# Down projection of an encoder layer: its DMA transfers put in an order written out by hand

## The chip, the core and the metric

The kernel runs on one core of a Trainium2 chip. The core has five engines with a queue of instructions each: TensorE (PE: matmuls, with its weight loads shown apart as PEld), VectorE (DVE), ScalarE (ACT), GpSimd (POOL) and SyncE (SP). SyncE computes nothing here; it issues DMA transfers, which a set of 16 DMA engines then carries out. The metric is the time of the whole program on the device in microseconds (us), lower is better. The kernel is built with a framework of tiles: the program says which tile an operation reads and writes, and a scheduler orders the instructions of each engine and places the semaphores. Where the program calls `tc.keep_in_program_order`, the scheduler keeps an instruction at its place in the program, relative to the others that are kept.

## The reference, cut to what matters

One layer of a streaming encoder on 512 prompt frames, 16 meta tokens and 64 sample frames, model width 2048, all in float32. The attention half (two head groups side by side, one output projection) is not touched here. What the change concerns is the second half:

```python
h = rmsnorm(x, lp['norm_ffn_g'])
x = x + (jax.nn.silu(h @ lp['ffn_w_gate']) * (h @ lp['ffn_w_up'])) @ lp['ffn_w_down']
...
y_prompt = rmsnorm(xp[:, N_META:], final_norm_g)
y_sample = rmsnorm(xs, final_norm_g)
```

Gate and up weights are 2048 x 5632, the down weights 5632 x 2048. After attention 576 tokens are left (`TQ`), which the kernel holds as two halves of 288 (`QH`).

## The kernel before, in words

*Number format.* A float32 product is made of three products of rounded parts (fp32r): each operand is split into a high part and a low part, and hi·hi, hi·lo and lo·hi are added up. A split takes ScalarE (copy to the high part: L156 for weights, L1185 for token operands) and then VectorE (what is left: L153 for weights, L1187 for operands).

*Seven products for eight.* The three big matmuls of the feed-forward use `winograd` (L998): blocks of 2 x 2 quarters are multiplied with 7 products, each of a sum of weight quarters (`ws`, L1025: some on GpSimd, one on VectorE) with a sum of token quarters. In the order `CHAIN` the first product takes a weight quarter as it is, so it needs only the two splits of `raw`. For each product TensorE runs `bh·wh` and `bl·wh` at L1056 and `bh·wl` at L1060. `wh` and `wl` have two buffers each, so ScalarE and VectorE prepare one product while TensorE runs another.

*Gate and up.* The loop `for u in range(FC // 2)` takes 22 units of 256 hidden columns. For each unit and each of gate and up, two weight pieces of 1 MB (`raw`) are loaded and the products are summed up in a tile `c` of the pool `fb`. At the end of a unit GpSimd multiplies gate and up (L1245, two instructions), the result is stored to DRAM (`actspill`, two stores of 288 KB), and for all units but the last two GpSimd also forms the four sums of quarters that the down projection needs, which are stored to `sumspill`.

*Down projection.* The 22 units are its contraction dimension, taken in `blocks = [4, 4, 4, 4, 4, 2]`. For each of the first five blocks there are 8 steps `d`, one for 256 output columns: `down_rows` loads a weight piece of 1 MB (`raw`, pool `fr`, two buffers), runs the 7 products (28 operands of 144 KB in all, held in SBUF in the pool `bc`), and VectorE adds each product into the accumulators `y` (L1295), which start with the residual, loaded from `x2spill` in the first block, two per step. The sixth block multiplies plainly (`plain_rows`), and behind it `finish` (two halves) normalises and turns the result: squares, the constant-setting of `vc`, a reciprocal root (`vc`, `rc`, L167 to L169), transposes on TensorE, scaling into `ot` by VectorE (L1348) or ScalarE (L1346), and the stores of the outputs.

*The operands of the next block.* `builder` (L1158) is a generator. It fetches operands `bl` from `actspill` and `sumspill`, a given number ahead, and converts them in two steps, ScalarE first, VectorE then. `down_rows` advances it once per product, so that three and a half operands become ready per step `d`, and a block's 28 during the block before. For the first block the same generator (`start`) is advanced by the last unit's "up" products; it is set to run 4 fetches ahead. What is left of it is drained behind the loop of units.

*What sets the order.* All loads and stores go through SyncE's one queue (L137, L140). From `pinned[0] = True` on (down projection), splits, sums and conversions are kept in program order by `pin`; the DMA transfers are not: the scheduler decides which goes first on SyncE's queue. The pool `yp`, from which the down projection takes `wh`, `wl` and `ws`, and the pool `yy` of the accumulators lie in memory that the gate/up pools (`fb`, `rw`, `fw`) give back, so that the first tiles of the down projection wait until the stores of the last `c` have read it.

Of the kernel before, what the change touches and what calls it, by code (L numbers as in the profile page):

```python
# [11 lines left out]
F32 = mybir.dt.float32  # L12
# [103 lines left out]
def encoder_step(  # L116
# [16 lines left out]

    S.preload_act_table_set("natural_log_exp_and_others")

    def load(dst, src):
        nc.sync.dma_start(dst, src)  # L137

    def store(dst, src):
        nc.sync.dma_start(dst, src)  # L140

    def const(name, shape, src):
        t = cp.tile(shape, F32, name=name)
# [844 lines left out]
    def load_raw(pool, src, r0, nk, c0, bufs, tag="raw"):  # L988
        r = pool.tile([P, nk, 256], F32, name="raw", tag=tag, bufs=bufs)
        load(r, src[r0:r0 + nk * P, c0:c0 + 256].rearrange("(k p) c -> p k c", p=P))  # L990
        return r
# [166 lines left out]
    def builder(m0, count, plain, ahead, by_product=False):  # L1158

        srcs = {}  # L1160
        for m in range(m0, m0 + count):
            quarter = [actspill[2 * m + f, :, c] for f in range(2) for c in (slice(0, QH), slice(QH, TQ))]
            if plain:
                for p, src in zip((1, 2, 4, 5), quarter):
                    srcs[m, p] = src
            else:
                for p, src in zip(ORDER, (quarter[0], quarter[2], sumspill[m, :, 2], sumspill[m, :, 0],
                                          sumspill[m, :, 1], quarter[3], sumspill[m, :, 3])):
                    srcs[m, p] = src
        order = [p for p, _ in CHAIN]  # L1170
        todo = sorted(srcs, key=lambda mp: order.index(mp[1])) if by_product else list(srcs)

        def fetch(n):
            for m, p in todo[n:n + 1]:
                hi = bc.tile([P, QH], F32R, name=f"bh{p}_{m % 8}")
                lo = bc.tile([P, QH], F32R, name=f"bl{p}_{m % 8}")
                load(f32(lo), srcs[m, p])
                operands[m % 8, p] = (hi, lo)

        for n in range(ahead):  # L1180
            fetch(n)
        for n, (m, p) in enumerate(todo):
            fetch(n + ahead)
            hi, lo = operands[m % 8, p]
            pin(S.activation(hi, f32(lo), AF.Copy))  # L1185
            yield
            pin(V.tensor_tensor(lo, f32(lo), f32(hi), op=ALU.subtract))  # L1187
            yield
# [14 lines left out]
            G.tensor_tensor(g[:, f, :], g[:, f, :], rb2, op=ALU.mult)  # L1203

    blocks = [4, 4, 4, 4, 4, 2]

    turn = 0
    norm = token_norm()
    start = builder(0, blocks[0], False, 4, True)
    for u in range(FC // 2):  # L1210
        out = {}
        for which, wsrc in (("g", w_gate), ("u", w_up)):
            first = turn == 0
            raws = []
            for hf in range(2):
                if turn:
                    rp, bufs = (rw, 1) if turn % 3 == 0 else (fr, 2)
                    raws.append(load_raw(rp, wsrc, hf * 1024, 8, u * 256, bufs))
                turn += 1
            c = fb.tile([P, 2, TQ], F32, name="c", tag="c" + which, bufs=2)  # L1220
            chain = () if first else CHAIN if u == FC // 2 - 1 and which == "u" else WIDE
            take = combined(*quarters(c[:, 0, :], c[:, 1, :]), chain)
            done = [0]

            def step():
                if u == 0 and which == "u":
                    next(norm, None)
                if u == FC // 2 - 1 and which == "u":
                    done[0] += 1
                    if done[0] > 2:  # L1230
                        for _ in range(2 * blocks[0]):
                            next(start, None)

            if first:
                winograd(fw, fb, raws, range(4, 8), take, banks0, step=step)
            else:
                winograd(fw, fb, raws, range(8), take, step=step, chain=chain)
            out[which] = c
            if u and which == "g":
                gated(c)  # L1240
        g, w = out["g"], out["u"]
        if u == 0:
            gated(g)
        for f in range(2):
            G.tensor_tensor(w[:, f, :], w[:, f, :], g[:, f, :], op=ALU.mult)  # L1245
            if u < FC // 2 - 1:
                store(actspill[2 * u + f], w[:, f, :])
        if u < FC // 2 - blocks[-1]:
            b11, b12, b21, b22 = quarters(w[:, 0, :], w[:, 1, :])
            t = g.rearrange("p f (h c) -> p (f h) c", h=2)  # L1250
            G.tensor_tensor(t[:, 0, :], b12, b11, op=ALU.subtract)
            G.tensor_tensor(t[:, 1, :], b22, t[:, 0, :], op=ALU.subtract)
            G.tensor_tensor(t[:, 2, :], b21, t[:, 1, :], op=ALU.subtract)
            G.tensor_tensor(t[:, 3, :], b22, b12, op=ALU.subtract)
            store(sumspill[u], t)
    for _ in start:
        pass
    for f in range(2):
        store(actspill[FC - 2 + f], out["u"][:, f, :])
    close_fb()  # L1260
    close_rw()
    yy, close_yy = pool("yy", "right")
# [23 lines left out]
                done(2 * d + f, h)  # L1286

    def down_rows(m0, n, d, slots, step):
        raws = [load_raw(fr, w_down, m0 * 256, 2 * n, d * 256, 2)]
        y11, y12, y21, y22 = quarters(y[2 * d], y[2 * d + 1])  # L1290
        parts = {1: (y11,), 5: (y22,), 6: (y12,), 2: (y11,), 7: (y22,), 3: (y12,), 4: (y21,)}

        def take(p, banks):
            for c in parts[p]:
                V.tensor_tensor(c, c, banks[p], op=ALU.add)  # L1295

        winograd(yp, yp, raws, slots, take, step=step, chain=CHAIN)
# [15 lines left out]
    def finish(h, ahead):  # L1313

        groups = [(q, j) for q in range(4) for j in range(3)]

        def turned(q, j):  # L1320
            o, n = tok[h][j]
            ps = pmt()
            for k in range(4):
                PE.transpose(ps[0:n, k * P:(k + 1) * P], y[q * 4 + k][:, o:o + n], ident)
            return ps

        held = []
        for g in groups[:ahead]:
            held.append(turned(*g))
            yield  # L1330
        pc = pmt()
        vc = yp.tile([P, 3], F32, name=f"vc{h}")
        rc = yp.tile([P, 3], F32, name=f"rc{h}")
        V.memset(vc, 1.0)
        for j, (o, n) in enumerate(tok[h]):
            PE.matmul(pc[0:n, 2 * j:2 * j + 2], sqs[h][:, o - h * QH:o - h * QH + n], ones[:, 0:2],
                      start=True, stop=True)
            V.tensor_scalar(vc[0:n, j:j + 1], pc[0:n, 2 * j:2 * j + 1], 1.0 / D, EPS, op0=ALU.mult, op1=ALU.add)
        rsqrt(rc, vc)
        yield  # L1340
        for i, (q, j) in enumerate(groups):
            o, n = tok[h][j]
            ps = held.pop(0) if held else turned(q, j)
            ot = yp.tile([P, 512], F32, name="ot", tag="ot", bufs=OT_BUFS)
            if i % 2:
                S.activation(ot[0:n], ps[0:n, :], AF.Copy, scale=rc[0:n, j:j + 1])  # L1346
            else:
                V.tensor_scalar(ot[0:n], ps[0:n, :], rc[0:n, j:j + 1], None, op0=ALU.mult)  # L1348
            cs = slice(q * 512, (q + 1) * 512)
            if o == 0:  # L1350
                store(y_sample[:, cs], ot[0:NS])
            else:
                store(y_prompt[o - NS:o - NS + n, cs], ot[0:n])
            yield

    pinned[0] = True
    first = 0
    for bi, n in enumerate(blocks):
        slots = [(first + k) % 8 for k in range(n)]
        if bi + 1 < len(blocks):  # L1360
            build = builder(first + n, blocks[bi + 1], bi + 2 == len(blocks), 4)

            def step():
                next(build, None)

            for d in range(KC // 2):
                if bi == 0:
                    for i in (2 * d, 2 * d + 1):
                        y.append(yy.tile([P, TQ], F32, name=f"y{i}"))
                        load(y[i], x2spill[i])  # L1370
                down_rows(first, n, d, slots, step)
            for _ in build:
                pass
        else:
            before = iter(())
            for h in range(2):
                for d in range(KC // 2):
                    plain_rows(first, n, d, (h,), slots, squares)
                    if d:
                        for _ in range(2):  # L1380
                            next(before, None)
                before = finish(h, 5 * h)
            for _ in before:
                pass
        first += n
# [78 lines left out]
```

## Time and profile before

| | us |
|---|---|
| the runs | 2552.08, 2550.22, 2552.07; median 2552.07 |
| the profiled execution | 2555.87 |
| span of its trace | 2554.1 |
| of it TensorE busy | 2452.2 |
| VectorE busy | 1800.2 |
| ScalarE busy | 1108.3 |
| GpSimd busy | 738.8 |

The span runs from the first to the last instruction on record; what lies around it (1.8 us) is start and end of the program. "Busy" counts an engine's computing instructions; DMA issues, semaphores and branches are left out. A group row of the page (`L1056 PE MATMUL m<-bh,wh ...`) names line, engine, operation, output and inputs, shapes and count, then busy time, the mean of one in ns, and the idle time just before such instructions with what ended it. A row of DMA issues names the transfer, the queue (`SPq` is SyncE's), its count, size, and the median time from issue to landing. In a timeline a row has the time from the start of the span, the duration, engine, line, operation, tiles and count; in square brackets stands how long the engine had waited and for what. The mean granted clock of TensorE was 0.986 of full speed in this execution.

### The profile page before, as it was taken

How to read it: one execution, taken by the hardware profiler on the slowest of the kernel's cores; microseconds unless marked ns; L12 is line 12 of the kernel's file. 1: busy time of each engine (PE TensorE's matmuls, PEld its weight loads, DVE VectorE, ACT ScalarE, POOL GpSimd, SP SyncE). 2: the span in 40 equal slices, each digit the busy share in tenths (PEclk: the TensorE clock that was granted, in tenths of full speed). 3: DMA queues.
4: the chain of work that ended last, by engine and by line, in shares of the span. 5: the costliest groups of instructions: out<-in, count | busy, mean ns of one | idle time of the engine just before them, and what ended most of it. 6: DMA issues, size and time to landing. Idle time of an engine off the chain costs nothing. (4 is left out here: it accounts for less than half of the span.)

```text
span 2554.1 us, 44879 instructions
## 1 busy us (share of the span) xinstructions
PE 2452.2 (96%) x17847; PEld 2393.5 (94%) x17847; DVE 1800.2 (70%) x2825; ACT 1108.3 (43%) x2008; POOL 738.8 (29%) x614
## 2 busy tenths in 40 slices
PE   6999999998999999999999999999999899999997
PEld 5999999987999888999999999999999899999997
DVE  5455555556555567877777777777777899899975
ACT  5233433334344444444444444444445444444445
POOL 0000000000000165554545445454543222222236
PEclk9999999999999899999999999999999899999999
DMA  6433223334232453343333334333335542452334
GB/s 205 123 92 97 80 80 85 86 87 140 88 96 84 140 157 124 118 137 116 121 104 127 128 118 137 114 121 105 128 127 166 201 153 83 151 162 83 108 102 149
DMA packets 330564, 307.73 MB, mean 120 GB/s; under 512 B 24708, under 2 KB 298507, under 8 KB 330355
## 3 DMA queue, kind: packets, MB, share of 16 engines
q1 hardware_dynamic: 330354, 304.87, 38.1%
q8 instruction: 140, 2.29, 0.4%
q14 instruction: 70, 0.57, 0.1%
HBM read 250.82 MB, written 56.68 MB: 120 GB/s over the span
## 5 line engine op out<-in xcount | busy, mean ns | idle before, releaser
L1056 PE MATMUL m<-bh,wh 128*128 128x288 f32 x3584 | 969.5, 296 | 13.4 <-DMA bl<-actspill 9.6
L1056 PE MATMUL m<-bl,wh 128*128 128x288 f32 x3584 | 969.0, 295 | 0.0
L1056 PEld LDWEIGHTS m<-bh,wh 128*128 128x128 f32 x3584 | 674.9, 188 | 14.4 <-ACT wh L156 14.3
L1056 PEld LDWEIGHTS m<-bl,wh 128*128 128x128 f32 x3584 | 678.6, 189 | 0.1
L1060 PE MATMUL m<-bh,wl 128*128 128x288 f32 x3584 | 586.4, 299 | 18.3 <-DVE wl L153 15.7
L1060 PEld LDWEIGHTS m<-bh,wl 128*128 128x128 f32 x3584 | 512.6, 189 | 32.3 <-DVE wl L153 31.3
L1025 POOL TENSOR_TENSOR ws<-raw 128x512 f32<-128x512 f32 x256 | 342.5, 1346 | 607.2 <-DVE wl L153 352.6
L156 ACT ACTIVATE wh<-ws 128x512 fp32r<-128x512 f32 (+1 forms) x340 | 288.8, 849 | 449.2 <-PE m L1056 300.4
L153 DVE TENSOR_TENSOR wl<-ws,wh 128x512 fp32r<-128x512 f32 (+1 forms) x340 | 379.9, 1117 | 114.1 <-ACT wh L156 113.6
L153 DVE TENSOR_TENSOR wl<-raw,wh 128x512 fp32r<-128x512 f32 x416 | 403.8, 985 | 27.1 <-ACT wh L156 17.2
L156 ACT ACTIVATE wh<-raw 128x512 fp32r<-128x512 f32 x416 | 249.7, 626 | 308.0 <-PE m L1056 279.3
L108 PE MATMUL ps<-xh,wh 128*128 128x296 f32 x992 | 229.3, 313 | 6.5 <-ACT wh L156 6.5
L108 PE MATMUL ps<-xl,wh 128*128 128x296 f32 x992 | 219.0, 302 | 0.0
L108 PE MATMUL ps<-xh,wl 128*128 128x296 f32 x992 | 218.7, 302 | 0.0
L108 PEld LDWEIGHTS ps<-xh,wh 128*128 128x128 f32 x992 | 163.4, 192 | 10.7 <-ACT wh L156 6.7
L108 PEld LDWEIGHTS ps<-xl,wh 128*128 128x128 f32 x992 | 164.1, 192 | 0.0
L108 PEld LDWEIGHTS ps<-xh,wl 128*128 128x128 f32 x992 | 163.8, 192 | 0.3 <-DVE wl L153 0.3
L1025 DVE TENSOR_TENSOR ws<-ws,raw 128x512 f32<-128x512 f32 x128 | 92.4, 722 | 87.4 <-POOL ws L1025 81.1
L153 DVE TENSOR_TENSOR wl<-wr,wh 128x1024 fp32r<-128x1024 f32 (+1 forms) x110 | 117.8, 1071 | 45.2 <-ACT wh L156 43.3
L1295 DVE TENSOR_TENSOR y<-y,m 128x288 f32<-128x288 f32 x280 | 125.5, 448 | 20.1 <-PE m L1060 18.8
L156 ACT ACTIVATE wh<-wr 128x1024 fp32r<-128x1024 f32 (+1 forms) x110 | 101.7, 929 | 80.3 <-PE ps L108 72.0
L1203 POOL TENSOR_TENSOR c<-c,rb 128x576 f32<-128x576 f32 x44 | 73.0, 1661 | 165.5 <-ACT c L1202 163.0
(363 smaller groups left out, 3330.2 us busy)
## 6 DMA issues: line engine op xcount, KB each, us to landing
raw<-in_ffn_w_gate SPq DMA_DIRECT2D x44, 1024.0 KB, 6.6
raw<-in_ffn_w_up SPq DMA_DIRECT2D x44, 1024.0 KB, 5.2
raw<-in_ffn_w_down SPq DMA_DIRECT2D x40, 1024.0 KB, 5.4
wr<-in_w_in SPq DMA_DIRECT2D x60, 512.0 KB, 4.0
actspill<-c SPq DMA_DIRECT2D x44, 288.0 KB, 2.1
sumspill<-c SPq DMA_DIRECT2D x20, 576.0 KB, 2.8
bl<-sumspill SPq DMA_DIRECT2D x80, 144.0 KB, 3.4
bl<-actspill SPq DMA_DIRECT2D x68, 144.0 KB, 3.8
```

What stands on the lines that cost most here:

```text
L108: self.tc.keep_in_program_order(self.pe.matmul(out, lhsT, rhs, start=start, stop=stop))
L153: V.tensor_tensor(lo, src, f32(hi), op=ALU.subtract)
L156: S.activation(hi, src, AF.Copy)
L1025: engine.tensor_tensor(w[:, k:k + m, :], pick(xs), pick(ys), op=op)
L1056: PE.matmul(banks[p], wh[:, k, :], x, start=first and new and k == 0 and x is hi, stop=False, skip_group_check=not new)
L1060: PE.matmul(banks[p], wl[:, k, :], hi, start=False, stop=last and k == n - 1, skip_group_check=not new)
L1203: G.tensor_tensor(g[:, f, :], g[:, f, :], rb2, op=ALU.mult)
L1295: V.tensor_tensor(c, c, banks[p], op=ALU.add)
```

## The change

- `load` and `store` become one function `transfer`, which keeps a transfer in program order on SyncE's queue while `paced[0]` is set. It is set at the first product of the last unit's "up" matmul and taken back at the beginning of the last block.
- The weight pieces of the down projection are asked for by `fetch_raw`, ahead of the step that uses them: the first within the last unit, the second behind the last operand of the first block, and each further one behind step `d - 2`. `down_rows` takes the piece from the dictionary `fetched`.
- `start` fetches 8 operands ahead instead of 4, in two groups of four: the first two steps of the last unit's "up" products each ask for one group.
- The last unit's two stores to `actspill` are issued by GpSimd (`G.dma_start`) instead of SyncE.
- The accumulators `y` are loaded four at the first step and then two per step, two steps ahead of their use.
- The constant-setting of `vc` in `finish` is kept in program order.

The arithmetic, its order on TensorE, and the sizes of the buffers stay as they are.

```diff
...
-    def load(dst, src):
-        nc.sync.dma_start(dst, src)
-
-    def store(dst, src):
-        nc.sync.dma_start(dst, src)
+    paced = [False]
+
+    def transfer(dst, src):
+        ins = nc.sync.dma_start(dst, src)
+        if paced[0]:
+            tc.keep_in_program_order(ins)
+
+    load = store = transfer
...
         for n in range(ahead):
             fetch(n)
+            if by_product and n % count == count - 1:
+                yield
         for n, (m, p) in enumerate(todo):
...
     blocks = [4, 4, 4, 4, 4, 2]
+    fetched = {}
+
+    def fetch_raw(m0, n, d):
+
+        fetched[m0, d] = load_raw(fr, w_down, m0 * 256, 2 * n, d * 256, 2)
 
     turn = 0
     norm = token_norm()
-    start = builder(0, blocks[0], False, 4, True)
+    start = builder(0, blocks[0], False, 2 * blocks[0], True)
...
                 if u == FC // 2 - 1 and which == "u":
                     done[0] += 1
+                    if done[0] == 1:
+                        paced[0] = True
+                        fetch_raw(0, blocks[0], 0)
+                    if done[0] < 3:
+                        next(start)
                     if done[0] > 2:
                         for _ in range(2 * blocks[0]):
                             next(start, None)
...
     for _ in start:
         pass
+    fetch_raw(0, blocks[0], 1)
     for f in range(2):
-        store(actspill[FC - 2 + f], out["u"][:, f, :])
+        G.dma_start(actspill[FC - 2 + f], out["u"][:, f, :])
...
     def down_rows(m0, n, d, slots, step):
-        raws = [load_raw(fr, w_down, m0 * 256, 2 * n, d * 256, 2)]
+        raws = [fetched.pop((m0, d))]
...
-        V.memset(vc, 1.0)
+        pin(V.memset(vc, 1.0))
...
+    def accumulator(i):
+        y.append(yy.tile([P, TQ], F32, name=f"y{i}"))
+        load(y[i], x2spill[i])
+
...
             for d in range(KC // 2):
-                if bi == 0:
-                    for i in (2 * d, 2 * d + 1):
-                        y.append(yy.tile([P, TQ], F32, name=f"y{i}"))
-                        load(y[i], x2spill[i])
+                if bi == 0 and d == 0:
+                    for i in range(4):
+                        accumulator(i)
+                if bi == 0 and 2 * d + 4 < KC:
+                    for i in (2 * d + 4, 2 * d + 5):
+                        accumulator(i)
                 down_rows(first, n, d, slots, step)
+                if d + 2 < KC // 2:
+                    fetch_raw(first, n, d + 2)
+                elif bi + 2 < len(blocks):
+                    fetch_raw(first + n, blocks[bi + 1], d + 2 - KC // 2)
             for _ in build:
                 pass
         else:
+            paced[0] = False
             before = iter(())
...
```

## The prediction

> **What bounds the kernel now.** I read the page first (busy shares, the slices, the groups), then the table of stretches over the down projection, then the timelines of the queues and engines where a stretch loses time.
>
> ```profile
> span 2554.1 us, 44879 instructions
> PE 2452.2 (96%) x17847; PEld 2393.5 (94%) x17847; DVE 1800.2 (70%) x2825; ACT 1108.3 (43%) x2008; POOL 738.8 (29%) x614
> L1056 PE MATMUL m<-bh,wh 128*128 128x288 f32 x3584 | 969.5, 296 | 13.4 <-DMA bl<-actspill 9.6
> raw<-in_ffn_w_down SPq DMA_DIRECT2D x40, 1024.0 KB, 5.4
> actspill<-c SPq DMA_DIRECT2D x44, 288.0 KB, 2.1
> bl<-sumspill SPq DMA_DIRECT2D x80, 144.0 KB, 3.4
> ```
>
> TensorE is the bound: 96% busy. Of the 13.4 us that it waits ahead of the first product of a group, 9.6 are one wait. The stretches place it:
>
> ```profile
> 1957.00:1978.00 21.00, 21.00 (x160) 21.00 (x160) 20.55 (x39) 16.41 (x36) 3.69 (x2) 1.00 0.88 263
> 1978.80:1984.10 5.30, 0.01 (x1) 0.00 (x0) 2.61 (x2) 0.41 (x1) 2.29 (x2) 1.00 0.96 312
> 1984.10:1988.40 4.30, 0.00 (x0) 0.00 (x0) 1.67 (x6) 2.17 (x6) 0.41 (x1) 0.50 0.70 236
> 1988.40:1997.80 9.40, 8.38 (x33) 8.04 (x34) 6.13 (x9) 2.55 (x5) 3.36 (x3) 0.50 0.96 331
> 1997.80:2003.60 5.80, 5.80 (x46) 5.80 (x45) 5.11 (x9) 3.20 (x6) 1.29 (x1) 1.00 0.30 105
> 2182.90:2196.90 14.00, 11.97 (x85) 11.26 (x85) 10.47 (x20) 5.32 (x10) 2.55 (x2) 1.00 0.66 209
> 2196.90:2365.00 168.10, 161.93 (x1177) 157.03 (x1178) 156.72 (x274) 78.50 (x148) 36.85 (x28) 1.00 0.36 113
> ```
>
> The columns are stretch, length, busy time of TensorE, its weight loads, VectorE, ScalarE and GpSimd, granted clock, DMA share, GB/s. Between the last unit and the first step of the down projection TensorE stands still for 9.6 us, then runs 9.4 us at half clock (33 products recorded, where 5.8 us at full clock hold 46). In the steady part VectorE, 156.7 of 168.1 us, is nearly as full as TensorE: 14 steps of 12.0 us. One step, 2182.9 to 2196.9, took 14.0. So three places can move: the seam, that step, and whatever the new queue order makes late.
>
> **The seam.** Timelines of SyncE's queue, GpSimd, ScalarE, TensorE and VectorE there:
>
> ```profile
> 1975.90 0.38 SPq L137 DMA_DIRECT2D raw<-in_ffn_w_down  x1
> 1976.38 3.79 SPq L137 DMA_DIRECT2D bl<-sumspill  x4
> 1980.27 1.27 SPq L140 DMA_DIRECT2D actspill<-c  x2
> ...
> 1978.02 3.07 POOL L1245 TENSOR_TENSOR c<-c 128x576 f32<-128x576 f32 x2 [14.37 <-issue]
> ...
> 1978.85 0.41 ACT L1131 ACTIVATE c<-m 128x288 f32<-128x288 f32 x1 [0.20 <-PE m L1060]
> 1985.10 1.54 ACT L1185 ACTIVATE bh<-bl 128x288 fp32r<-128x288 f32 x4 [5.84 <-DMA bl<-sumspill]
> 1987.76 0.63 ACT L156 ACTIVATE wh<-raw 128x512 fp32r<-128x512 f32 x1 [1.13 <-DMA actspill<-c]
> ...
> 1988.44 0.61 PE L1056 MATMUL m<-bh,wh 128*128 128x288 f32 x1 [9.63 <-DMA bl<-actspill]
> 1991.70 0.61 PE L1060 MATMUL m<-bh,wl 128*128 128x288 f32 x1 [0.97 <-DVE wl L153]
> ...
> 1977.80 3.60 DVE L1187 TENSOR_TENSOR bl<-bl,bh 128x288 fp32r<-128x288 f32 x3
> 1985.57 1.58 DVE L1187 TENSOR_TENSOR bl<-bl,bh 128x288 fp32r<-128x288 f32 x4 [4.17 <-ACT bh L1185]
> ```
>
> The wait is put down to an operand, but ScalarE's rows tell what came last: the first weight split (1987.76) waits until the last unit's products `c` have been stored, since `wh` of the new pool lies where `c` was. The second store was issued at about 1981.1 and landed at about 1987.7: 6.6 us, where such stores take 2.1 by the page. Ahead of it on the queue stood a weight piece of 1 MB and four operands; those too landed late (1985.1).
>
> **The change, part by part, against the profiled execution (2555.87 us).**
>
> *Stores on GpSimd's queue, block 1's operands and the second weight piece behind block 0's operands.* The order of instructions in the changed kernel: multiplication, store, multiplication, store on GpSimd; ScalarE's last copy of `c` now stands behind two of the last four conversions. Without the weight piece these operands, released at 1976 as now, land some 2.2 to 3.4 us later, so the copy ends near 1979.6 instead of 1979.26. First multiplication done at 1979.55 (half of 3.07). No row shows a store issued by GpSimd; SyncE's two took 0.64 each at this place, and I take that, from 0.3 to 2.1 (a whole landing). The second multiplication runs 1980.2 to 1981.75, 0.65 later than before; its issue ends at 1982.4. Landing: 2.1 at best, 6.6 at worst if it again waits its turn; the weight piece, now issued near 1978 and landing 5.4 later at 1983.4, is still being moved, so I take 2.1 plus some 0.4: 1984.9. The split starts 2.9 us earlier than at 1987.76. Ends: 4.5 earlier (no delay, 2.1) to 1.5 later. Behind the split nothing comes sooner: the operands then land near 1980.5, GpSimd's sum and VectorE's subtraction wait for the same stores. **-2.9 (-4.5 to +1.5).**
>
> For the store's price the Trainium skill has a figure (DMA: Bandwidth & Descriptors, Anatomy of one DMA, SWDGE path): about 2.0 us plus bytes over 436 GB/s per DMA of GpSimd, by which I estimate 2.7 us for 288 KB and the seam at -2.7; no run here shows it yet.
>
> *Half clock.* The wait stays near 6.7 us, and the clock had been cut 5.3 us into it. It came back 9.4 after the restart, 6.1 after the second wait (1991.70). I keep 9.4. If the clock comes back 3.4 us sooner or later (the length that 1984.1 to 1997.8, 13.7, holds four times), half of it counts: **0 (-1.7 to +1.7).**
>
> *The step of 14.0 us.* Its rows:
>
> ```profile
> 2182.90 0.38 SPq L137 DMA_DIRECT2D raw<-in_ffn_w_down  x1
> 2183.37 2.90 SPq L137 DMA_DIRECT2D bl<-sumspill  x3
> ...
> 2186.38 0.63 ACT L156 ACTIVATE wh<-raw 128x512 fp32r<-128x512 f32 x1 [0.63 <-PE m L1056]
> 2188.02 0.63 ACT L156 ACTIVATE wh<-ws 128x512 fp32r<-128x512 f32 x1 [1.01 <-PE m L1056]
> 2191.81 0.44 ACT L1185 ACTIVATE bh<-bl 128x288 fp32r<-128x288 f32 x1 [3.15 <-DMA bl<-sumspill]
> ...
> 2192.82 0.69 DVE L1025 TENSOR_TENSOR ws<-ws,raw 128x512 f32<-128x512 f32 x1 [3.25 <-POOL ws L1025]
> ```
>
> A cluster of operands surrounded the weight piece; both came late, ScalarE and VectorE waited. In the new order three or four operands follow each piece and none is in flight ahead of it. Back to 12.0: **-2.0 (-2.0 to 0).** The weight pieces themselves come no earlier: there are two buffers in both kernels, and a piece already leaves when its buffer is free (2182.90, 2196.89); "two steps ahead" is what the trace shows already. That part counts 0.
>
> *First operands of a block.* The scheduler used to load them before the block began. Pinned, they stand behind the weight piece issued at a block's start, and the first conversion follows in the same step. ScalarE gets there 4.1 us into the step (2186.38 + 0.63 - 2182.90). The operand leaves 0.5 in. By its own 3.4 it lands at 3.9 and costs nothing; behind the piece (5.4) at some 6.0; at worst as above, 8.9. At 6.0 two conversions of 0.43 push the next split from 5.1 to 6.9; TensorE wants its 0.63 us finished at about 7.0, late by 0.5. Four blocks (the first has the seam's slack): **+2.0 (0 to 8.2, four times the 2.05 of the step above).**
>
> *Tail.* The constant-setting of `vc` is pinned, and the scheduler puts two weight splits behind the normalisation and two output scalings:
>
> ```profile
> 2515.93 0.68 DVE L153 TENSOR_TENSOR wl<-raw,wh 128x512 fp32r<-128x512 f32 x1
> 2516.53 0.15 DVE L169 SCALAR_TENSOR_TENSOR rc<-vc,rc 128x3 f32<-128x3 f32 x1
> 2516.72 1.40 DVE L1348 TENSOR_SCALAR ot<-m,rc 64x512 f32<-64x512 f32 x2
> ```
>
> One split moves behind 1.40 us of scalings; transposes moved forward on TensorE cover most: **+0.4 (-0.6 to +1.4).** The loads of `y`, spread over the steps, cost nothing: each is due two steps, 24 us, later. Without that cover a pair would add about its 1.1 us of issue and landing.
>
> Sum: -2.9 + 0 - 2.0 + 2.0 + 0.4 = **-2.5 us**; ends -8.8 and +12.8. The profiled execution, 2555.87, is 3.8 above the median 2552.07; taken from the median: **2549.6 us.**
>
> **The rivals.**
>
> *The seam closes further* (faster). Store landed at the low end (-4.5), clock back one length sooner (-1.7), the long step gone (-2.0), the block starts hidden because VectorE sets the pace there anyway (0): -8.2, 2543.9. For it: 156.7 of 168.1 on VectorE, so a late ScalarE split has some room; against it: the new store sits in line on GpSimd between two multiplications.
>
> *Operands late at each block's start* (slower). One mechanism: ScalarE takes its work in order, and a conversion waiting for its operand holds every weight split behind it. At 3.15 per block, the wait in the row of 2191.81, four cost 12.6 instead of 2.0: +8.1, 2560.2. With the rest as forecast it decides from 2.4 a block. Against: other weight pieces land within 5.4, which leaves most of a split's slack.
>
> *The stores are no quicker on the other queue.* They need the same DMA engines, and the weight piece is still under way: landing 6.6 again, at 1989.0, so +1.2 at the seam, sum +1.6, 2553.7. For it: 312 GB/s in that stretch, DMA share 0.96. Against: the new order takes a megabyte and thirteen operands from ahead of them.
>
> *VectorE holds the stores up.* Its three subtractions beside the multiplications took 3.60, 1.2 each, against 1.58 for four afterwards: the two engines get in each other's way. If GpSimd must wait for VectorE's last subtractions before a store can go, and these end near 1983, the store lands 1.5 later: sum -1.0, 2551.1. The Trainium skill (SBUF — State Buffer, SBUF: two separate sides) warns of just that: GpSimd's DMA descriptors cannot be written while VectorE holds the shared port in a fast mode. Whether these subtractions use that mode no run here shows.
>
> **How the numbers follow.** Chances: forecast 0.37, further closing 0.34, late operands 0.18, stores no quicker 0.07, VectorE in the way 0.04. I take 0.2%, 5.1 us, as what can be told from no change. The first, fourth and fifth lie within it: 0.48; faster 0.34; slower 0.18. The range reaches down past the rival to the sum's lower end, 2552.07 - 8.8 = 2543, and up to where slower begins, 2557, which leaves out the 0.18.
>
> **What would show it.** Right: the wait ahead of the first product of the down projection near 6.7 us, ended by a store of GpSimd's, its first weight split 2.9 us closer behind the last unit; the half-clock stretch still there; no step of 14 us; short waits of ScalarE for operands at block starts. Wrong: the half clock gone, GpSimd's issue or landing much over 3 us, waits for operands of 2 us or more in four steps, or steps that differ from 12.0 throughout.

## The result, and the profile after

Over 11 runs each the changed kernel takes 2558.66 us in the median, the kernel before 2552.63. The ratio is 1.0022, with a 95% interval of 1.0014 to 1.0030: by the ratio 5.6 us slower, between 3.6 and 7.7. The forecast was 2.5 us faster (2549.6 us, from 2543 to 2557). The profiled execution took 2559.38 us.

The page of the changed kernel has nearly the same busy times as before:

```profile
span 2557.1 us, 44837 instructions
PE 2449.7 (96%) x17847; PEld 2390.5 (93%) x17847; DVE 1800.2 (70%) x2825; ACT 1106.9 (43%) x2008; POOL 739.8 (29%) x616
L1059 PE MATMUL m<-bh,wh 128*128 128x288 f32 x3584 | 968.4, 296 | 13.1 <-ACT wh L159 9.7
bl<-sumspill SPq DMA_DIRECT2D x80, 144.0 KB, 5.0
```

TensorE's waits ahead of the first products of a group come to 13.1 us in place of 13.4, 9.7 of them now put down to weight splits, and the operands take 5.0 us to land where they took 3.4. The stretches of the changed kernel (columns as in the prediction): seam, the start of the fourth block, and the end from the thirteenth weight piece of the last block on:

```profile
1978.90:1983.90 5.00, 0.15 (x2) 0.00 (x0) 4.41 (x5) 1.52 (x4) 3.96 (x4) 1.00 0.89 295
1983.90:1986.10 2.20, 0.00 (x0) 0.00 (x0) 0.00 (x0) 0.63 (x1) 0.52 (x1) 0.50 0.35 134
1986.10:1994.10 8.00, 7.09 (x28) 6.75 (x29) 5.28 (x8) 1.89 (x3) 3.27 (x3) 0.50 0.95 311
...
2277.07:2290.62 13.55, 11.64 (x85) 11.20 (x85) 10.86 (x20) 5.74 (x11) 2.56 (x2) 1.00 0.52 166
...
2508.80:2557.10 48.30, 33.96 (x239) 31.23 (x239) 23.03 (x47) 25.35 (x43) 20.46 (x25) 0.86 0.45 142
```

The same block start and the same end in the first profile of the kernel before:

```profile
2280.26:2292.19 11.93, 11.65 (x85) 11.19 (x85) 10.47 (x20) 5.43 (x10) 2.73 (x2) 1.00 0.74 231
...
2510.18:2554.10 43.92, 32.57 (x237) 29.75 (x237) 22.01 (x45) 25.40 (x42) 21.30 (x25) 0.92 0.49 156
```

TensorE's idle at the seam is 7.2 us instead of 9.6, where the forecast was near 6.7. The block start has 13.55 us instead of 11.93, and the end 48.30 instead of 43.92. So the seam gave a little, and two places that the prediction had priced at +2.0 and +0.4 took more.

**The seam, changed kernel.** GpSimd, ScalarE and TensorE:

```profile
1982.92 0.58 POOL L1275 DMA_DIRECT2D actspill<-c  x1 [0.31 <-POOL c L1260]
...
1985.46 0.63 ACT L159 ACTIVATE wh<-raw 128x512 fp32r<-128x512 f32 x1 [4.59 <-DMA actspill<-c]
...
1986.15 0.61 PE L1059 MATMUL m<-bh,wh 128*128 128x288 f32 x1 [7.10 <-ACT wh L159]
```

As forecast, a store of GpSimd's ends the wait of the first weight split.

**Start of the fourth block, changed kernel.** Timelines of SyncE's queue, ScalarE, VectorE and TensorE:

```profile
2277.07 0.38 SPq L139 DMA_DIRECT2D raw<-in_ffn_w_down  x1
2277.54 2.69 SPq L139 DMA_DIRECT2D bl<-actspill  x2
...
2280.53 0.63 ACT L159 ACTIVATE wh<-raw 128x512 fp32r<-128x512 f32 x1 [0.96 <-PE m L1059]
2284.15 0.83 ACT L1190 ACTIVATE bh<-bl 128x288 fp32r<-128x288 f32 x2 [2.98 <-DMA bl<-actspill]
...
2284.63 0.87 DVE L1192 TENSOR_TENSOR bl<-bl,bh 128x288 fp32r<-128x288 f32 x1 [2.50 <-ACT bh L1190]
...
2286.01 0.37 PE L1059 MATMUL m<-bh,wh 128*128 128x288 f32 x1 [1.78 <-ACT bh L1190]
```

The first operands are issued behind the weight piece. ScalarE waits 2.98 us for them, VectorE 2.50 for ScalarE, and TensorE stands still for 1.78. ScalarE's waits over all the steps, in the table of waits (total, number of times, longest):

```profile
ACT bh L1190 <- DMA bl<-actspill: 8.2, 4, 3.0
```

Four waits, one for each block start (1.8, 1.7, 3.0 and 1.8 us). In the kernel before, where the long one is the step of 14.0 us:

```profile
ACT bh L1185 <- DMA bl<-sumspill: 4.8, 3, 3.1
```

**The end, changed kernel.** SyncE's queue, ScalarE and TensorE:

```profile
2508.81 0.37 SPq L139 DMA_DIRECT2D raw<-in_ffn_w_down  x1
2515.75 3.25 SPq L139 DMA_DIRECT2D out<-ot  x4
2519.10 0.54 SPq L139 DMA_DIRECT2D raw<-in_ffn_w_down  x1
2519.88 0.36 SPq L139 DMA_DIRECT2D out<-ot  x1
2520.59 0.38 SPq L139 DMA_DIRECT2D raw<-in_ffn_w_down  x1
...
2525.08 0.63 ACT L159 ACTIVATE wh<-raw 128x512 fp32r<-128x512 f32 x1 [2.66 <-DMA raw<-in_ffn_w_down]
...
2525.77 0.40 PE L192 MATMUL m<-bh,wh 128*128 128x288 f32 x1 [2.69 <-ACT wh L159]
```

SyncE's queue before:

```profile
2510.18 6.83 SPq L137 DMA_DIRECT2D raw<-in_ffn_w_down  x2
2517.49 3.77 SPq L140 DMA_DIRECT2D out<-ot  x4
2521.36 0.53 SPq L137 DMA_DIRECT2D raw<-in_ffn_w_down  x1
```

Before, the fourteenth weight piece of the last block goes ahead of four output stores (the second of the two in the first row, issued at 2516.65); after, it goes behind them, at 2519.10, with the next piece 1.5 us behind it, and TensorE waits 2.69 us. No edit touched these transfers.

### The profile page after: what moved, and what is told of

Its sections match the earlier page's. It is cut to its first block, busy times and chain, and to the rows that moved or that the text cites. A ratio compares the mean times of both kernels' runs of the same rounds, so it can differ in the third digit from the quotient of the medians.

```text
span 2557.1 us, 44837 instructions
## 1 busy us (share of the span) xinstructions
PE 2449.7 (96%) x17847; PEld 2390.5 (93%) x17847; DVE 1800.2 (70%) x2825; ACT 1106.9 (43%) x2008; POOL 739.8 (29%) x616
## 5 line engine op out<-in xcount | busy, mean ns | idle before, releaser
L1059 PE MATMUL m<-bh,wh 128*128 128x288 f32 x3584 | 968.4, 296 | 13.1 <-ACT wh L159 9.7
```

Of the source, the lines that this page charges most:

```text
L1059: PE.matmul(banks[p], wh[:, k, :], x, start=first and new and k == 0 and x is hi, stop=False, skip_group_check=not new)
```

## The experiments

Beside the medians, a few times (in us) are read from each trace: the first weight split counted from the start of the last gate/up product (seam), the sum of the first steps of blocks 2 to 5, each from one weight piece's issue to the next (starts), and the time from the eleventh weight piece of the last block to the end of the span (end). A single execution scatters by some 2 us, so the ratios decide and the traces tell the place. The runs come from several chips, and each ratio is to runs of the kernel before on the same one; medians of different runs are therefore not compared as they stand.

| kernel | ratio to before, 95% interval | seam | starts | end |
|---|---|---|---|---|
| before, first profile | 1 | 9.2 | 49.4 | 52.0 |
| before, once more | (2551.04 us, one run) | 8.1 | 47.5 | 52.1 |
| pin of vc alone | 1.0013 [1.0004, 1.0023] | 8.3 | 49.2 | 54.1 |
| change, not paced | 1.0014 [1.0005, 1.0022] | 9.5 | 48.1 | 53.9 |
| change | 1.0022 [1.0014, 1.0030] | 6.7 | 50.6 | 56.4 |
| change, no pin of vc | 1.0021 [1.0011, 1.0030] | 8.6 | 51.3 | 52.7 |
| change, stores on SyncE | 1.0030 [1.0019, 1.0041] | 8.1 | 49.9 | 54.2 |
| change, no pin, first operands early | 1.0006 [0.9997, 1.0015] | 8.1 | 46.8 | 52.4 |
| change, both mended | 0.9998 [0.9989, 1.0007] | 8.5 | 47.0 | 51.6 |

### The pin of vc undone, and alone

```diff
-        pin(V.memset(vc, 1.0))
+        V.memset(vc, 1.0)
```

> The changed kernel with one edit undone: the constant-setting of vc is not kept in program order. In the order of instructions SyncE's queue in the tail then reads as before the change (two weight pieces, four stores of ot, a piece, three stores, a piece) instead of a piece, four stores, a piece, one store, a piece, two stores, a piece. Theory A (the pin of vc put a weight piece behind four output stores, and that is the 4.4 us which the tail lost between the two profiles): 2558.7 - 4.4 = 2554.3 us, and ScalarE's wait of 2.66 us for a weight piece in the tail is gone. Rival B (the tail lost by a late landing, by chance, or by the order in the blocks before): 2558.7 us.

```diff
-        V.memset(vc, 1.0)
+        pin(V.memset(vc, 1.0))
```

> The kernel before with that one edit alone: the constant-setting of vc kept in program order. Theory A (the pin alone makes the loss in the tail): 2552.6 + 4.4 = 2557.0 us, with the tail's order of the changed kernel. Rival B (the pin is harmless, the loss belongs to the rest of the change): 2552.6 us.

Measured: 2557.37 us without the pin, 2555.62 with the pin alone (before, beside them: 2551.68). The queue's order follows the pin in both directions. SyncE's queue and ScalarE in the kernel before with the pin alone:

```profile
2516.10 3.01 SPq L140 DMA_DIRECT2D out<-ot  x4
2519.21 0.54 SPq L137 DMA_DIRECT2D raw<-in_ffn_w_down  x1
...
2524.56 0.63 ACT L156 ACTIVATE wh<-raw 128x512 fp32r<-128x512 f32 x1 [1.79 <-DMA raw<-in_ffn_w_down]
```

and in the changed kernel without it:

```profile
2511.34 6.83 SPq L139 DMA_DIRECT2D raw<-in_ffn_w_down  x2
2518.65 3.77 SPq L139 DMA_DIRECT2D out<-ot  x4
2522.51 0.53 SPq L139 DMA_DIRECT2D raw<-in_ffn_w_down  x1
```

Theory A has the right mechanism and the wrong size. The end takes 51.6 to 52.7 us in the five profiles of the table without the pin in the tail and 53.9 to 56.4 in the four with it: some 2 us, of which the first profile of the change showed an unlucky 4.4 (two pieces in flight together, and a half-clock stretch of 3.4 us behind the wait). Alone the pin costs 0.13% (1 to 6 us). Taken out of the change it brought only 0.01%, uncertain by some 3 us on either side; that is short of A's 4.4 and does not exclude 2.

### Not paced

```diff
-                        paced[0] = True
+                        paced[0] = False
```

> The changed kernel with its transfers never kept in program order; all else stays, the stores on GpSimd's queue and the pin of vc too. The whole loss is 6.0 us; with 3.0 gained at the seam and 4.4 lost in the tail, 4.6 are left for the blocks. Theory C (the blocks lose by the order written out by hand, since each block's first operands stand behind a weight piece; the gain at the seam belongs to GpSimd's queue): 2558.7 - 4.6 = 2554.1 us, block starts without ScalarE's waits for operands. Theory D (the gain at the seam belongs to the order too, since it takes a megabyte out of the stores' way): 2554.1 + 3.0 = 2557.1 us. Rival E (the order is not what costs the blocks): 2558.7 us.

Measured: 2554.4 us. Against the kernel before beside it that is 3.6 us slower by the ratio (1.3 to 5.6), between theory C (2554.1 against 2552.6, 1.5 slower) and theory D (4.5); the time alone decides neither, and only rival E (6.1) lies outside. The trace tells more. The four block starts are back at 48.1 us, as theory C had it, so the order costs the starts. What is left of the loss (0.14%) is about that of the pin alone, which this kernel still has. But theory D is right on the seam: with the stores on GpSimd's queue and the old order, the first split is as late as ever. GpSimd and ScalarE in this kernel:

```profile
1981.80 0.71 POOL L1275 DMA_DIRECT2D actspill<-c  x1 [0.31 <-POOL c L1260]
1984.24 0.58 POOL L1275 DMA_DIRECT2D actspill<-c  x1 [0.31 <-DMA bl<-sumspill]
...
1988.84 0.63 ACT L159 ACTIVATE wh<-raw 128x512 fp32r<-128x512 f32 x1 [2.97 <-DMA actspill<-c]
```

The second store leaves 4.9 us after the last product, where SyncE sent it after 2.6, and lands 4.5 us later.

### The stores on SyncE's queue

```diff
-        G.dma_start(actspill[FC - 2 + f], out["u"][:, f, :])
+        store(actspill[FC - 2 + f], out["u"][:, f, :])
```

> The changed kernel with the last unit's two stores given back to SyncE's queue, in program order, so that they stand behind the second weight piece and ahead of the accumulators. Theory F (GpSimd's queue lets the stores go sooner): the first weight split of the down projection comes as late as before the change, 3 us later, 2561.7 us. Theory D (what helped was that the operands ahead were fewer; the queue does not matter): within 1 us of 2558.7.

Measured: 2559.61 us. By the ratios that is some 2 us more than the change (1.0030 against 1.0022), uncertain by 3.5, so the time excludes neither theory D (no more) nor theory F (3 us more). In the trace the split comes 8.1 us after the last product; with GpSimd's queue it came at 6.7, 8.6, 8.1 and 8.5 in four profiles. SyncE issues the second store 3.5 us after the last product, and it lands 4.4 us later; GpSimd issues it after 3.9 to 5.6, behind its multiplication and the 0.71 us of its first issue, and it lands 2.4 us later in two of the four and 4.4 in the others. The queue is worth nothing that these runs can tell.

### The kernel before, once more

> The kernel before, unchanged, for a second profile. Its first profiled execution was 3.8 us above its median, the changed kernel's 0.7 above. Theory I (the step of 14 us at a block's start and the length of the half-clock stretch are luck of one execution): this one shows neither at the same place, and its span is nearer 2550. Rival J (they belong to the kernel): both are there again, the step within 0.3 us.

Measured: 2551.04 us. The stretch table for the first step of the third block, which had 14.0 us in the first profile:

```profile
2180.79:2192.71 11.92, 11.68 (x85) 11.21 (x85) 11.55 (x20) 5.54 (x10) 2.59 (x2) 1.00 0.75 243
```

The long step is gone, as theory I said; the half-clock stretch at the seam is as long as before (13.7 us, and 10.2 to 17.1 in the other kernels). The long step turned up in two of the four kernels whose transfers the scheduler orders (14.0, 13.9, 11.9, 11.9 at this step), both times with the weight piece late among the operands (its last packet 8.1 and 8.0 us after its issue), and in none of the paced ones (12.3, 12.4, 12.3). The unpaced changed kernel has a milder one at the fourth block (13.0 us, ScalarE waiting 2.13 for an operand).

### The first operands of a block early

```diff
-        for n in range(ahead):
-            fetch(n)
-            if by_product and n % count == count - 1:
+        for n in range(ahead):
+            fetch(n)
+            if by_product and n % count == count - 1 or early and n == 1:
                 yield
...
+                at[0] += 1
+                if at[0] == 7 * (KC // 2) - 1 and bi + 2 < len(blocks):
+                    queued[0] = builder(first + n + blocks[bi + 1], blocks[bi + 2], bi + 3 == len(blocks), 4, early=True)
+                    next(queued[0])
```

(beside it, the pin of vc is undone)

> The changed kernel without the pin of vc, and with the first two operands of each block fetched within the last step of the block before, ahead of the weight piece behind which they stood. Theory C (each block start loses some 0.5 us, and more where its weight piece is late, because ScalarE waits for these operands with the weight splits queued behind): the steps at block starts go from 12.3 to 11.9, the late one from 13.9 to 12.3 at most, ScalarE's waits for operands are gone: 2557.4 - 2.8 = 2554.6 us. Rival E (the block starts are late by their weight pieces alone): 2557.4 us, steps unchanged.

Measured: 2553.44 us, ratio 1.0006, where the same kernel with late operands has 1.0021: 3.8 us, uncertain by 3.3. Theory C holds, with more than it asked for: the four starts fall from 51.3 to 46.8 us. The start that had taken 13.9, in the stretch table:

```profile
2275.74:2287.78 12.04, 11.67 (x85) 11.20 (x85) 10.55 (x20) 5.43 (x10) 2.58 (x2) 1.00 0.50 163
```

and ScalarE's waits for operands in all steps, first with late operands, then with early ones:

```profile
ACT bh L1190 <- DMA bl<-actspill: 8.6, 4, 3.3
...
ACT bh L1190 <- DMA bl<-sumspill: 1.0, 2, 0.9
```

8.6 us in four waits have become 1.0 in two.

### Both mended

The first operands early, and `vc` set in the third block in place of the tail:

```diff
+        if bi == 2:
+            for h in range(2):
+                vcs.append(yp.tile([P, 3], F32, name=f"vc{h}"))
+                pin(V.memset(vcs[h], 1.0))
...
-        vc = yp.tile([P, 3], F32, name=f"vc{h}")
...
-        pin(V.memset(vc, 1.0))
+        vc = vcs[h]
```

> The changed kernel with the first two operands of each block fetched early, as in the run before, and with vc set in the middle of the down projection (third block) in place of the tail: so neither the tail's queue order changes nor does VectorE stand at the seam behind the stores. Theory K (the change loses at the block starts, some 3.9 us by the run with early operands, and in the tail, some 2 us by the profiles with and without the pin; otherwise it is worth about -1 at the seam): 2558.7 - 3.9 - 2.0 = 2552.8 us, the time before. Rival L (a good part of the loss lies elsewhere): 2555 us or more.

Measured: 2552.93 us, ratio 0.9998 [0.9989, 1.0007]. Theory K: with the block starts and the tail mended the whole loss is gone, and so, nearly, is any gain.

### What holds the seam

The pool `yp` holds `wh`, `wl`, `ws` and, at its end, the tail's `ot`. The first three lie where the gate/up pool `fw` was; `ot` lies over the last `c`. Here `ot`, `vc` and `rc` get a pool of their own, in the kernel before:

```diff
     yp, close_yp = pool("yp")
+    yo, close_yo = pool("yo")
...
-            ot = yp.tile([P, 512], F32, name="ot", tag="ot", bufs=OT_BUFS)
+            ot = yo.tile([P, 512], F32, name="ot", tag="ot", bufs=OT_BUFS)
```

> The kernel before with one edit: ot, vc and rc of the tail are taken from a pool of their own. The pool yp then has 14336 bytes per partition in place of 22636 and no longer reaches into the memory of the last c; wh, wl and ws keep their addresses, none of which c ever had. Theory G (the first weight split waits for the stores only because the pool as a whole overlaps c): the wait of 9.6 us ahead of the first product falls to 3 at most, and with no long wait the clock is not cut: 2552 - 6.6 - 4.7 (half of the 9.4 us at half clock) = 2540.7 us. Rival H (the operands, which ScalarE converted from 1985.10 on, and the weight piece would have been late just the same): the wait moves to them, 2552 - 2.7 (1987.76 - 1985.10) = 2549.3 us.

Measured: 2551.36 us, ratio 0.9999 [0.9990, 1.0008]. In its profile the first split no longer waits for the stores: it starts 0.3 us behind the last copy of `c`. So it was the pool's reach that had held it, and not, as the prediction had it, the place of `wh` itself. But TensorE then waits 3.6 us for VectorE's half of the split and 2.1 for the accumulators, which still wait for the stores. In the profile the seam, from the last gate/up product to the issue of the third weight piece, takes 21.5 us, against 25.1 and 24.0 in the two profiles of the kernel before: a gain of 2.5 to 3.6 us. In the times there is none that the interval shows (2.6 us faster to 2.0 slower). Neither G nor H forecast that. The profiled execution, 2545.18 us, was the fastest of this kernel, and some 3 us of its lead stand ahead of the seam already (its last up piece is issued at 1939.9, against 1943.6 and 1942.6 in the two profiles of before); whether the timed runs keep the gain at the seam stays open.

The same together with the changed order, without the pin of vc, first operands early:

> The changed kernel without the pin of vc, with the first operands of a block early and with ot, vc and rc in their own pool. Theories C and G: 2554.6 - 11.3 + 2.9 (what the change had gained at the seam already) = 2546 us, or less if nothing but the wait for the stores had kept the order by need from paying. Rival H: 2554.6 us, since the order has the operands there early already.

Measured: 2550.47 us, 0.9994 [0.9985, 1.0003]: by the ratios 3 us less than without the pool (1.0006), uncertain by as much, and short of the 8.4 that theory G took off.

Next the accumulators were freed too: the first four `y` in a pool that lies where `rw` was, `vc` set in the third block. First on the kernel before:

```diff
+    ya, close_ya = pool("ya", "right")
     yy, close_yy = pool("yy", "right")
...
-                        y.append(yy.tile([P, TQ], F32, name=f"y{i}"))
+                        y.append((ya if i < 4 else yy).tile([P, TQ], F32, name=f"y{i}"))
```

> The kernel before with the same freed seam, but nothing of the change: ot, vc, rc in their own pool, the first four y in a pool of their own, vc set in the third block; the order of transfers and of products left to the scheduler as before. Theory G: 2552 - 7 = 2545 us (24 us at the seam become 17, since the scheduler puts a sum ahead of the first split on VectorE). Rival M: 2551 us.

Measured: 2548.66 us, ratio 0.9983 [0.9974, 0.9992], the fastest of all and faster than both kernels: 4.3 us less than before (2.0 to 6.6), of theory G's 7. In the profile the seam takes 19.0 us. TensorE stands still for 3.6 us of the stretch below, beside a busy VectorE and GpSimd:

```profile
1977.20:1981.10 3.90, 0.30 (x4) 0.07 (x2) 3.90 (x3) 2.13 (x6) 3.90 (x3) 0.82 0.93 311
```

Then the same seam on the mended change, with the first step's products and VectorE's work in it in a fixed order:

```diff
+    EARLY = ((1, "a"), (2, "c"), (5, "b"), (6, "a"), (7, "a"), (3, "b"), (4, "a"))
...
-        winograd(yp, yp, raws, slots, take, step=step, chain=CHAIN)
+        strict[0] = m0 == 0 and d == 0
+        winograd(yp, yp, raws, slots, take, step=step, chain=EARLY if strict[0] else CHAIN)
+        strict[0] = False
```

(`strict` keeps VectorE's splits and sums in program order; the second weight piece is asked for behind the first four `y`)

> That kernel, with what holds TensorE at the seam taken away: ot, vc, rc in their own pool; the first four accumulators y in a pool of their own that lies where rw was and not over c, loaded ahead of the second weight piece; and in the first step the products of plain weights first (1, 2, 5, 6, 7, 3, 4), with VectorE's splits and sums kept in that order. Theory G (the stores were all that held the seam): from the last gate/up product to the third weight piece 24 us become 15 (a step of 12 and some 3 of idle), no half clock in between: 2552.8 - 9 = 2544 us. Rival M (GpSimd's two multiplications and VectorE's sums get in each other's way there; the profile of the run with all three had VectorE's 0.69 us sum at 3.08 beside them): 18.7 us as in that run, 2550 us.

Measured: 2562.67 us, 1.0034 [1.0022, 1.0047], slower by 9 us or so, and neither theory has it. VectorE and GpSimd at the seam of this kernel:

```profile
1979.50 5.48 DVE L1200 TENSOR_TENSOR bl<-bl,bh 128x288 fp32r<-128x288 f32 x4 [0.17 <-ACT bh L1198]
1984.91 2.12 DVE L158 TENSOR_TENSOR wl<-raw,wh 128x512 fp32r<-128x512 f32 x1
...
1978.36 2.24 POOL L1268 TENSOR_TENSOR c<-c 128x576 f32<-128x576 f32 x1 [14.20 <-issue]
1980.91 0.71 POOL L1282 DMA_DIRECT2D actspill<-c  x1 [0.31 <-POOL c L1268]
1981.64 1.30 POOL L1034 TENSOR_TENSOR ws<-raw 128x512 f32<-128x512 f32 x1
1982.89 1.40 POOL L1268 TENSOR_TENSOR c<-c 128x576 f32<-128x576 f32 x1
```

Four subtractions that take 1.58 us alone (in the prediction's rows) take 5.48 beside GpSimd, and the split behind them 2.12 instead of 0.68. From there on the splits stood in the fixed order behind additions to `y` that wait for TensorE (2.4 to 2.7 us for most of them), and TensorE waited four more times, for 0.6 to 4.4 us. Without the fixed order:

> The mended kernel with the freed seam (the pools of ot and of the first four y, and these four loaded ahead of the second weight piece), but with the first step's products and VectorE's order left as they were. Theory N (the run before it lost its 9 us by the order held on VectorE alone, where each split stands behind an addition that waits for a product of TensorE): the seam is again near 19 us and the time 2552.9 - 4.4 = 2548.5 us, as for the same seam in the kernel before; so the order by need adds nothing to the freed seam. Rival O (y loaded early or the stores on GpSimd's queue did it): 2558 us or more.

Measured: 2551.0 us, 0.9995 [0.9986, 1.0004]. The 9 us are gone, so the fixed order did the harm (that of the products or that of VectorE's work: the two were not parted), and rival O's 2558 is excluded. But theory N's time is missed by 2.5 us, and its seam too: it takes 22.2 us here, where the kernel before with the same pools took 19.0. (The 18.7 us that an expectation above gives for the run with all three counts from the product ahead of TensorE's longest wait, which already belongs to the down projection; from the last gate/up product that run took 21.6.) VectorE and TensorE at this seam:

```profile
1983.59 3.09 DVE L1028 TENSOR_TENSOR ws<-ws,raw 128x512 f32<-128x512 f32 x1 [3.61 <-POOL ws L1028]
1986.96 0.68 DVE L156 TENSOR_TENSOR wl<-raw,wh 128x512 fp32r<-128x512 f32 x1
...
1987.70 1.33 PE L1063 MATMUL m<-bh,wl 128*128 128x288 f32 x4 [5.18 <-DVE wl L156]
```

TensorE waits 5.18 us for a split that stands behind a sum, and the sum waits for GpSimd's, which is ready 5.3 us after the last gate/up product; in the kernel before with the same pools it is ready after 2.5: there the multiplication ahead of it takes 1.50 us and not 2.98, and no issue of a store (0.71) stands between. So with the freed seam, too, the change adds nothing: 0.9983 without it, 0.9995 with it.

## Why the prediction was wrong, by its own steps

The forecast failed in four terms of its sum, all in the same direction: the two gains (seam -2.9, long step -2.0) were worth about 1 us each, and the two costs (block starts +2.0, tail +0.4) about 3 and 2.

*The seam, -2.9.* That the first weight split waits for the stores was right; the reason, that `wh` lies where `c` was, was not (its pool reaches there, with tiles used much later). The first profile showed nearly the forecast size: 6.7 us from the last product to the first split in place of 9.2. It was luck. Over the four profiles with the scheduler's order the split comes at 9.2, 8.1, 8.3 and 9.5, over the three of the change and its two undone edits at 6.7, 8.6 and 8.1. The means differ by 1.0 us. And the gain comes from the order, not from GpSimd's queue.

*GpSimd's price and the weight piece beside it.* The issues cost 0.71 and 0.58 us, the value taken (0.64). The second store's landing, taken as 2.5, was 2.4 us in two of the table's five profiles with GpSimd's stores (the change; first operands early) and 4.4 to 4.5 in the three others. By the figure of the Trainium skill (DMA: Bandwidth & Descriptors, Anatomy of one DMA, SWDGE path) the prediction had estimated 2.7; the first two come near it, the others do not. What the term had wrong is the second weight piece, which it let land 5.4 us after its issue. In the profile of the change it did; in the four other paced profiles of the table it took 7.0 to 7.8 us. Where the piece had moved its last packet by the end of GpSimd's second issue (the change; first operands early), the store took the 2.4; where it was moving for 2.1 us more (no pin of vc; both mended), the store took the 4.4.

*Half clock, 0.* Right: it did not go, and its length (10.2 to 17.1 us in the profiles) follows no edit.

*The step of 14.0 us, -2.0.* This step failed too. The 14.0 us were seen in one profiled execution that ran 3.8 us above the median, and its gain was taken off the median, which holds it only at times. In the second profile of the same kernel the step takes 11.9 us. The reading of the row was right (operands around a weight piece; no paced kernel shows it), but its worth against the median is about 1 us, two executions in four, and not 2.

*First operands of a block, +2.0.* The mechanism was right, the size too small. In the profile of the change, ScalarE gets its operands 5.8 to 5.9 us into the step at three of the four starts, the 6.0 of the forecast, and these steps take 12.3 to 12.4 us, some 0.5 more than in the kernel before, as forecast. At the fourth block they come after 7.1 us, and TensorE's share is 1.78 instead of 0.5: the piece ahead is itself late in one step out of three (below), which the term did not have. In the traces the starts cost 3 us; mending them is worth 3.8 us by the ratios (1.0021 against 1.0006, uncertain by 3.3) and 4.5 in the traces, 0.7 of them beyond the scheduler's own order.

*Tail, +0.4.* This step failed most plainly. It counted the work that the pin moves on VectorE, and not the queue that the scheduler orders anew for it: with the pin, a weight piece goes behind four output stores on SyncE's queue, and TensorE waits 1.5 to 2.7 us for it in the four profiles. The term measured some +2.

*The sum.* In the traces: -1 (seam), -1 (long step), +3 (starts: 50.6 us in the mean of the three paced kernels, 47.5 in the four others with the long step set to 11.9), +2 (tail): 3 us of the measured 5.6 (3.6 to 7.7). Mending the last two brings the kernel to 0.9998 of before, so that the loss lies there; the 2 us or so that the traces do not show are within what single executions scatter, and stay unplaced. By the ratios the pin alone is worth 3.3 us and the starts 3.8, which would cover the whole, but each is uncertain by some 3 us. The rival "operands late at each block's start", which had named 2.4 us a block as the point from which it decides, came nearest in kind, at 0.8 to 1.1 us a block; that little sufficed because the two gains on the other side were half of what they had been taken for, and the tail cost 2 us more.

*VectorE holds the stores up*, the rival of 0.04: in part. GpSimd's issues were not held up (0.31 us behind its multiplications in the table's five profiles with GpSimd's stores), but the first multiplication was: beside VectorE's subtractions it took 2.2 to 3.0 us, where it took 1.50 in the kernel before. That puts the stores 0.7 to 1.5 us later; the rival had 1.5. It goes the other way round too, as the run with the fixed order shows: of its four subtractions two took 0.45 us each, the others 1.42 and 3.40, and both of these ended 0.32 us behind an instruction of GpSimd's. The Trainium skill (SBUF — State Buffer, SBUF: two separate sides) says that an operation of VectorE with two inputs in SBUF and one of GpSimd that reads SBUF shut each other out for a whole instruction; the 5.48 us against 1.58 agree.

## What to carry to other kernels

A wait seen once in one profiled execution is not a term against a median: profile the kernel twice before counting on its removal. When one instruction is pinned under a scheduler, compare the order of every queue, far from the edit too; here a pin of 0.06 us of work moved a weight piece of half a megabyte behind four stores. And when transfers are put in order by hand, what a block needs first must stand ahead of the large piece that is not needed yet.

## What the hardware showed beside

In the nine profiles of the table, 12 of the 38 weight pieces from the third one to the end of the fifth block have a 16 KB packet of the instruction queue (q8 on the page) begin within 5 us of their issue; such packets come some 18 us apart. These pieces have moved their last packet 6.0 to 6.3 us after their issue (the median of each profile), the others 4.85; the landing that the page counts comes some 0.5 later. A packet of the instruction queue is under way for 1.1 to 1.4 us (medians), about what these pieces lose. So the program's own instructions, on their way to an engine, seem to hold up a weight piece at every third step, the same steps in all nine profiles; no run varied this, so the cause is argued from the times alone. The fourth block's start of the changed kernel, 13.55 us, is such a step: its piece is issued at 2277.1, the packet begins at 2278.2, and the piece's last packet has gone 6.2 us after its issue.
